# A hybrid attention and GLA layer on one core: the side work moved to another stretch of the product stream, and the blocks of x put first

## The chip, the cores and the metric

The kernel runs on one core of one Trainium2 chip. The metric is the device time of one execution in microseconds (us); the median of three runs before the change is 1817.47 us (1816.67 to 1818.06). A difference of under 0.2% (3.6 us) is taken as no change.

## What is computed

One layer, 2048 prompt tokens and 8 sequences of 8 new tokens (2112 tokens of width 1024). One wide projection gives the inputs of two branches, a sliding-window attention and a gated linear attention (GLA). Each branch is gated, projected to 1024, scaled by a sigmoid gate, and the sum is projected and normalised.

```python
z = jnp.einsum('btd,dn->btn', x, w_in)
q, k, v, g_att, gq, gk, gv, g_gla, g_lr, r_att, r_gla = jnp.split(z, SPLIT_POINTS, axis=-1)
...
    o_att = swa_prompt(q, k, v, attn_sink, rel_table)
...
log_a = jax.nn.log_sigmoid((jnp.einsum('btr,rk->btk', g_lr, w_gk_up) + b_gk)) / GATE_NORMALIZER
o_gla, S = gla(gq * HK ** -0.5, gk, gv, log_a, s0)      # causal, with a state S that is carried on
o_gla = o_gla * lax.rsqrt(jnp.mean(jnp.square(o_gla), -1, keepdims=True) + EPS) * gla_norm_w
h_att = jnp.einsum('bta,ad->btd', o_att * jax.nn.silu(g_att), w_pa)
h_gla = jnp.einsum('btv,vd->btd', o_gla * jax.nn.silu(g_gla), w_pg)
merged = jax.nn.sigmoid(r_att) * h_att + jax.nn.sigmoid(r_gla) * h_gla
y = jnp.einsum('btd,de->bte', merged, w_o)
x = layer_norm(DN_ALPHA * x + y, ln_g, ln_b)
```

## The kernel before

**Products.** The tokens are cut into three blocks (s = 0, 1, 2) of two halves of 352. Every big product is made of fp32r matmuls: each operand is split into a high and a low part (`split`, lines 141 to 145: ScalarE copies, VectorE subtracts), and `hi*hi + hi*lo + lo*hi` is three matmuls (lines 1300 to 1302). The wide projection is done in 2x2 blocks with seven products in place of eight (`ORDER`, line 50); sums of weight blocks are made on GpSimd (`tt`, line 339), sums of x blocks on VectorE (`mix`, line 452), and the partial results are put together by VectorE and ScalarE in `combine` (line 364). In block s = 0 all split weights are made here and four of seven are stored to DRAM (line 362); later blocks load those (line 319).

**Sets and the count of products.** The stream of products is a list of sets, `seq` (line 251): `x0, x1, x2` are the wide projection of a token block (177, 175 and 175 products), `a0..a2` the attention's gated projection (16 product lengths each) and `u0..u2` the GLA's (32 each). A product here is four times three matmuls of 352 columns. `base` holds the number of the product at which a set begins. The order before is x0 (0), x1 (177), a0 (352), u0 (368), x2 (400), a1 (575), u1 (591), a2 (623), u2 (639); at 671 the last projection and the norm follow.

**Side work.** Attention and GLA run between products. `at(t, fn)` (line 124) puts a step behind product t, and `tick` (line 127) runs the steps when that product has been issued. TensorE's order is this written order; the instructions of the other engines, which take their work in order too, are placed by a scheduler. `att_phase(s, t0)` (line 938) does the attention blocks of token block s, one every seven products: loads (`att_load`, line 722), the transposes of v (`att_prep`, line 748), the scores, the transposes of the weights, and the output. `gla_phase(s, t0, t1)` (line 1156) does the GLA in units of 128 tokens of a head, spread evenly over what lies between t0 and t1. A unit takes a PSUM tile `pa` (line 76) five times, of four that rotate: two transposes and scores (`gla_v`, `gla_a`), `gla_c` a third of a unit later, and two in `gla_b` at two thirds. The output of `gla_b` is held until `gla_norm` (line 1068) has been through ScalarE (the square, line 1072), GpSimd (lines 1073 and 1074) and ScalarE again (line 1075).

Before the change attention 0 begins at product 32 and GLA 0 at 80; attention 1 at 207, GLA 1 at 262; attention 2 at 430, GLA 2 at 487 to 636. The units stand 4.93, 5.73 and 5.01 products apart, from line 1161, for example (207 - 80 - 14 - 3) / (20 + 7/3) = 4.93.

**Operands of x.** `Ops.steps` (line 454) loads the four blocks of x and makes the seven split operands; `XOFF` and the other tables (lines 501 to 507) say at which product, counted from the start of the set, each step is issued. The operands live in sixteen rotating buffers `xb`, so a load waits until an operand of the set before has been used for the last time. `lowrank` (line 526) multiplies the four raw blocks with the small matrix of the GLA gate on TensorE (line 533); before, it stood in step `s7`.

Of the kernel before, what the change touches and what calls it, by code (L numbers as in the profile page):

```python
# [21 lines left out]
P = 128  # L22
# [14 lines left out]
GH = 4  # L37
# [6 lines left out]
MS = NT // (2 * MT)  # L44
# [13 lines left out]
def kernel(ctx, tc, io):  # L58
# [189 lines left out]
    px_pairs = [cx[j:j + 2] for j in range(0, 16, 2)] + [cx[16:]] + [cr[j:j + 2] for j in range(0, 8, 2)]  # L248
    two = lambda q: [[(q, 0), (q, 1)], [(q, 2), (q, 3)]]
    how = {"x": (4, px_pairs), "a": (2, two(PA_)), "u": (4, two(PG_))}  # L250
    seq = ("x0", "x1", "a0", "u0", "x2", "a1", "u1", "a2", "u2")
    sets = [(k[0], int(k[1])) + how[k[0]] for k in seq]

    groups, start_of, base = [], [], []
# [30 lines left out]
        tk += (len(groups) - start_of[-1]) * kh / 4  # L285
    start_of.append(len(groups))
    base.append(int(tk))
    X0, X1, A0, U0, X2, A1, U1, A2, U2 = range(9)
    XS = (X0, X1, X2)


# [118 lines left out]
    class Ops:  # L410
# [43 lines left out]
        def steps(self):  # L454
            r = self.r

            def s0():
                self.load(0, 0, 4 if self.n == X0 else 1)
                self.load(0, 1)

            def s1():
                self.make(1, r[0, 0], 4 if self.n == X0 else 2)

            def s2():
                self.load(1, 1)
                self.c = mtile("xb", name="cx")[:, :self.kh * T]
                self.mix(self.c, r[1, 1], r[0, 1], ALU.subtract)

            def s3():
                self.make(7, self.c)  # L470

            def s4():
                self.mix(self.c, self.c, r[0, 0], ALU.add)
                self.make(6, self.c)

            def s5():
                self.load(1, 0)

            def s6():
                self.mix(self.c, r[1, 0], self.c, ALU.subtract)  # L480
                self.make(4, self.c)

            def s7():
                if self.kind == "x":
                    lowrank(self)
                self.mix(r[0, 1], r[0, 1], r[0, 0], ALU.subtract)
                self.make(5, r[0, 1])

            def s8():
                self.make(2, r[1, 0])  # L490

            def s9():
                self.make(3, r[1, 1])

            if seq[self.n] in PLAIN:
                ld = lambda k, t: lambda: self.load(k, t)
                mk = lambda k, t: lambda: self.make((k, t), r[k, t])
                return (ld(0, 0), ld(0, 1), mk(0, 0), mk(0, 1), ld(1, 0), ld(1, 1), mk(1, 0), mk(1, 1))
            return s0, s1, s2, s3, s4, s5, s6, s7, s8, s9

    XOFF = (-18, -13, -11, -9, -7, -6, -3, 0, 1, 2)
    AOFF = (-30, -28, -24, -18, -13, -10, -6, -4, -2, 0)
    UOFF = (-16, -15, -12, -9, -4, -3, -1, 1, 2, 3)
    PX = (-18, -17, -12, -10, -8, -7, -6, -4)
    PA = (-28, -26, -24, -20, -18, -16, -12, -8)
    PU = (-16, -15, -12, -10, -8, -7, -5, -3)
# [107 lines left out]
    SU = 13  # L614
# [71 lines left out]

    at(SU, later(setup0))
    for h in range(0, NH, 2):
        at(SU + 3 + h, later(lambda h=h: setup1(h)))
    at(SU + 3, later(setup2))  # L690
    at(SU + 12, later(setup4))
    at(SU + 17, setup5)

    def gate_load(B):
        x = B["x"] = mtile("fin", name="gin")
# [242 lines left out]
    def att_phase(s, t0):  # L938
        at(t0, lambda: mpool(f"ca{s}"))
        at(t0, setup3)  # L940
        bl = ABL[s]
        for j, b in enumerate(bl):
            o = t0 + 8 + j * SB
            at(o - 7, lambda b=b: att_load(b))
            at(o - 7, lambda b=b: att_q(b))
            at(o - 1, lambda b=b: att_prep(b))
            at(o, lambda b=b: att_scores(b, 0))
            at(o, lambda b=b: att_scores(b, 2))
            at(o + 5, lambda b=b: att_sil(b))
            at(o + 6, lambda b=b: att_trans(b, 0))  # L950
            at(o + 6, lambda b=b: att_trans(b, 1))
            at(o + 9, lambda b=b: att_out(b))
        o = t0 + 8 + len(bl) * SB
        if s < MS - 1:
            return o + 5
        at(o - 4, samp_load)
        at(o + 1, samp_q)
        at(o + 2, samp_keys)
        at(o + 3, samp_rows)
        at(o + 4, lambda: samp_scores(0))  # L960
        at(o + 5, lambda: samp_scores(1))
        at(o + 9, lambda: samp_trans(0))
        at(o + 10, lambda: samp_trans(1))
        at(o + 12, samp_out)
        return o + 14
# [165 lines left out]
    def samp_b(B, j0):  # L1131
# [16 lines left out]
        for q in range(2):  # L1148
# [4 lines left out]
                                               sp[q][:, j * HV:(j + 1) * HV], ALU.mult, ALU.add)  # L1153
            b = 4 * q + j0
            nc.sync.dma_start(io["o_ss"][b:b + 2, B["h"]].rearrange("b k v -> k b v"), S0)
    def gla_phase(s, t0, t1):
        at(t0, lambda: mpool(f"cg{s}"))
        at(t0, rings)
        nu = sum(-(-T_ // P) for _, T_ in GCH[s]) * GH
        b0 = t0 + 14  # L1160
        st = (t1 - b0 - 3) / (nu + 7 / 3)
        u = 0
        for h, (c0, T_) in ([(h, c) for c in GCH[s] for h in range(GH)] if s == 1 else
                            [(h, c) for h in range(GH) for c in GCH[s]]):
            if True:
# [5 lines left out]
                b = tt(u)  # L1171
# [22 lines left out]
                    at(max(o + 6, tt(u + 4 / 3) + 1), lambda B=B: gla_store(B))  # L1194
                else:
                    at(tt(u + 7 / 3) + 1, lambda B=B: gla_store(B))

    for s in range(MS):
        for t in range(2):
            B = dict(s=s, t=t)  # L1200
            g0 = base[XS[s]] + (22 + 4 * t if s == 0 else 7 + 7 * t)
            at(g0 - 5, lambda B=B: gate_load(B))
            at(g0, lambda B=B: gate(B, 0))
            at(g0 + (s > 0), lambda B=B: gate(B, 2))
            at(g0 + 3 * (s > 0), lambda B=B: gate_end(B))
    e = att_phase(0, 32)
    for s in range(MS):
        t1 = base[XS[s + 1]] + 30 if s < MS - 1 else base[U2] - 3
        gla_phase(s, e, t1)
        if s < MS - 1:  # L1210
            e = att_phase(s + 1, t1)
    at(base[U2] + 1, lambda: mpool("cm"))


# [343 lines left out]
```

## Time and profile before

| what | value |
|---|---|
| median of the runs | 1817.47 us |
| the profiled execution, its own time | 1812.49 us |
| its span, first to last instruction | 1810.7 us |
| TensorE busy | 1767.8 us (98%) |
| VectorE, ScalarE, GpSimd busy | 1060.0, 839.0, 334.8 us |
| DMA | 452 MB, 250 GB/s on average |

The profile gives busy time per engine, waits with what ended them, and the same by stretches of time. A stretch is tied to the program by counting the matmuls of line 1300: four of them are one product of the wide projection. TensorE is the engine to watch: what it waits for is lost, and what others wait for is lost only if TensorE waits behind it. Line numbers up to 483 are the same in both kernels; behind that those of the changed kernel are 2 or 3 lower.

### The profile page before, as it was taken

The page shows a single profiled execution, that of the slowest core. Times are in us where ns is not written, and L with a number is a line of the kernel's source. Part 1 is how long each engine was busy: PE and PEld are TensorE (multiplying, and loading weights), DVE is VectorE, ACT ScalarE, POOL GpSimd, SP SyncE. Part 2 cuts the span into 40 slices and gives each one's busy share as a digit, 9 for nine tenths or more (in the row PEclk, how much of TensorE's full clock was granted, in tenths as well). Part 3 has the DMA queues.
Part 4 walks back from the last instruction along what each step waited for, and adds up shares of the span by engine and source line. Part 5 has one row for each costly group of instructions (what it writes and reads, how often), then busy time and mean ns, then how long its engine had stood idle before and what let it go on. Part 6 is the DMA issues. An engine that isn't in the chain of part 4 may idle for free.

```text
span 1810.7 us, 31028 instructions
## 1 busy us (share of the span) xinstructions
PE 1767.8 (98%) x10850; PEld 1652.0 (91%) x10850; DVE 1060.0 (59%) x2077; ACT 839.0 (46%) x1987; POOL 334.8 (18%) x473
## 2 busy tenths in 40 slices
PE   8999999998999999999999999999999999999997
PEld 8888999997898899999999998899999999998886
DVE  7577677767546654545666446554446744536665
ACT  5856555555745553445434746544445432311100
POOL 5333344554200000000034000000000022021111
PEclk9999999999999999999999999999999999999999
DMA  6789587977698779788986797788879987975531
GB/s 218 253 300 325 202 312 279 316 255 250 211 310 278 235 240 295 258 279 276 319 221 138 263 327 222 225 277 303 285 249 321 309 231 205 325 153 193 170 102 53
DMA packets 291053, 452.03 MB, mean 250 GB/s; under 512 B 29694, under 2 KB 210230, under 8 KB 290881
## 3 DMA queue, kind: packets, MB, share of 16 engines
q1 hardware_dynamic: 263536, 416.27, 69.4%
q10 hardware_dynamic: 19536, 24.47, 3.8%
q0 software_dynamic: 7824, 9.31, 3.6%
q8 instruction: 86, 1.41, 0.3%
q14 instruction: 71, 0.57, 0.1%
HBM read 297.52 MB, written 153.30 MB: 249 GB/s over the span
## 4 chain that ended last, share of the span: by engine, by line
PE 80%; DMA 6%; DVE 4%; ACT 3%; POOL 3%; issue 3%; SPq 1%; DVEq 0%; ACTq 0%; POOLq 0%
PE pd L1300 19%; PE pd L1302 18%; PE pd L1301 18%; PE pd L1364 3%; PE pd L1363 3%; PE pd L1365 3%; POOL ws L339 2%; PE pa L813 1%; PE pa L1087 1%; PE pa L1088 1%; PE pa L799 1%; PE pa L767 1%; PE pa L1085 1%; DVE wp L143 1%; DMA ws<-w_g 1%
## 5 line engine op out<-in xcount | busy, mean ns | idle before, releaser
L143 DVE TENSOR_TENSOR wp<-ws,wp 128x512 fp32r<-128x512 f32 (+1 forms) x396 | 268.7, 684 | 218.2 <-ACT wp L142 199.2
L142 ACT CAST wp<-ws 128x512 fp32r<-128x512 f32 (+1 forms) x396 | 233.0, 594 | 198.1 <-PE pd L1302 126.1
L339 POOL TENSOR_TENSOR ws<-ws 128x256 f32<-128x256 f32 x162 | 140.3, 899 | 157.9 <-DVE wp L143 111.2
L1073 POOL TENSOR_SCALAR sq<-sq 128x1 f32<-128x1 f32 x68 | 21.8, 321 | 721.8 <-ACT on L1072 721.5
L1300 PE MATMUL pd<-x7h,wp 128*128 128x352 f32 x292 | 98.6, 338 | 4.7 <-ACT fin L186 3.7
L375 ACT COPY m<-pd 128x352 f32<-128x352 f32 x146 | 65.4, 451 | 78.3 <-PE pd L1302 77.7
L1364 PE MATMUL pd<-woh,x 128*128 128x512 f32 x256 | 100.0, 391 | 0.0
L1363 PE MATMUL pd<-woh,x 128*128 128x512 f32 x256 | 99.8, 390 | 0.0
L1365 PE MATMUL pd<-wol,x 128*128 128x512 f32 x256 | 99.5, 389 | 0.0
L1300 PE MATMUL pd<-x1h,wp 128*128 128x352 f32 x292 | 97.5, 334 | 1.9 <-ACT gb L1030 1.9
L1300 PE MATMUL pd<-x2h,wp 128*128 128x352 f32 x292 | 98.2, 336 | 0.0
L1300 PE MATMUL pd<-x3h,wp 128*128 128x352 f32 x292 | 97.6, 334 | 0.6 <-DVE fin L390 0.6
L1300 PE MATMUL pd<-x4h,wp 128*128 128x352 f32 x292 | 97.6, 334 | 0.0
L1300 PE MATMUL pd<-x6h,wp 128*128 128x352 f32 x292 | 97.3, 333 | 0.0
L1300 PE MATMUL pd<-x5h,wp 128*128 128x352 f32 x292 | 96.7, 331 | 0.2 <-ACT u L379 0.2
L1302 PE MATMUL pd<-x7h,wp 128*128 128x352 f32 x292 | 94.8, 325 | 1.6 <-DVE wp L143 1.6
L1302 PE MATMUL pd<-x1h,wp 128*128 128x352 f32 x292 | 94.9, 325 | 0.0
L1301 PE MATMUL pd<-x1l,wp 128*128 128x352 f32 x292 | 94.8, 325 | 0.0
L1301 PE MATMUL pd<-x7l,wp 128*128 128x352 f32 x292 | 94.7, 324 | 0.0
L1301 PE MATMUL pd<-x3l,wp 128*128 128x352 f32 x292 | 94.6, 324 | 0.0
L1302 PE MATMUL pd<-x3h,wp 128*128 128x352 f32 x292 | 94.6, 324 | 0.0
L1302 PE MATMUL pd<-x6h,wp 128*128 128x352 f32 x292 | 94.2, 323 | 0.0
(441 smaller groups left out, 5263.2 us busy)
## 6 DMA issues: line engine op xcount, KB each, us to landing
wp<-wk_w_g SPq DMA_DIRECT2D x96, 512.0 KB
ws<-w_g SPq DMA_DIRECT2D x120, 256.0 KB
wk_w_g<-wp SPq DMA_DIRECT2D x48, 512.0 KB
wp<-wk_w_ra SPq DMA_DIRECT2D x32, 512.0 KB
wp<-wk_w_rg SPq DMA_DIRECT2D x32, 512.0 KB
ws<-w_at SPq DMA_DIRECT2D x54, 256.0 KB
wp<-wk_w_at SPq DMA_DIRECT2D x24, 512.0 KB
ws<-w_pg SPq DMA_DIRECT2D x48, 256.0 KB
```

Source lines behind the costliest of these rows:

```text
L142: pin["a"] = nc.scalar.copy(dst_h, src)
L143: i = eng.tensor_tensor(dst_l, src, dst_h.bitcast(F32), ALU.subtract)
L339: nc.gpsimd.tensor_tensor(o[:, c], x[:, c], y[:, c], op)
L375: nc.scalar.copy(A[i], ps)
L767: mm(ps[kv][:, j, k0:], A["zq"][r, g0 + j, :], A["kk"][r, 0, k0:], start=True, stop=True, tile_position=(kv * HD, 0))
L1073: nc.gpsimd.tensor_scalar(sq[:n], sq[:n], EPS, None, op0=ALU.add)
L1300: mm(ps, wh, xh[:, ts], start=first, stop=False, skip_group_check=ch)
L1301: mm(ps, wh, xl[:, ts], start=False, stop=False, skip_group_check=ch)
L1302: mm(ps, wl, xh[:, ts], start=False, stop=(k == q.kh - 1 and not (type(i) is tuple and i[1] == 0)), skip_group_check=ch)
L1363: mm(ps, xh[:, xs], hi, start=(k == 0), stop=False)
L1364: mm(ps, xl[:, xs], hi, start=False, stop=False)
L1365: mm(ps, xh[:, xs], lo, start=False, stop=(k == KT - 1))
```

## The change

- `seq`: x2 now stands ahead of a0 and u0: x0 (0), x1 (177), x2 (352), a0 (527), u0 (543), a1 (575), u1 (591), a2 (623), u2 (639).
- Side work: attention 0 begins at product 90 in place of 32, and all GLA units of the three blocks have one distance, (636 - 90 - 160 - 51) / 75 = 4.47 products. By that, attention 0 begins at 90, GLA 0 at 138, attention 1 at 254, GLA 1 at 309, attention 2 at 443, GLA 2 at 500 (to 634).
- The setup of the bias and the first two gates stand further apart (gates at 40 and 52 in place of 22 and 26).
- `att_prep` stands three products ahead of the scores in place of one; the load of `kk` stays seven ahead.
- `XOFF`: the seven operands of x1 and x2 are made later and further apart; `lowrank` moves to 2 products ahead of the set (from the set's first product), while the load of the last raw block moves from 6 to 3 ahead.

```diff
-    seq = ("x0", "x1", "a0", "u0", "x2", "a1", "u1", "a2", "u2")
+    seq = ("x0", "x1", "x2", "a0", "u0", "a1", "u1", "a2", "u2")
...
             def s7():
-                if self.kind == "x":
-                    lowrank(self)
                 self.mix(r[0, 1], r[0, 1], r[0, 0], ALU.subtract)
                 self.make(5, r[0, 1])
...
-            return s0, s1, s2, s3, s4, s5, s6, s7, s8, s9
-
-    XOFF = (-18, -13, -11, -9, -7, -6, -3, 0, 1, 2)
-    AOFF = (-30, -28, -24, -18, -13, -10, -6, -4, -2, 0)
-    UOFF = (-16, -15, -12, -9, -4, -3, -1, 1, 2, 3)
+            return s0, s1, s2, s3, s4, s5, s6, s7, s8, s9, lambda: lowrank(self)
+
+    XOFF = (-18, -12, -9, -6, -4, -3, 0, 3, 5, 7, -2)
+    AOFF = (-30, -28, -24, -18, -13, -10, -6, -4, -2, 0, -5)
+    UOFF = (-16, -13, -10, -7, -4, -3, 0, 3, 5, 7, -2)
...
-        at(SU + 3 + h, later(lambda h=h: setup1(h)))
+        at(SU + 5 + 4 * h, later(lambda h=h: setup1(h)))
     at(SU + 3, later(setup2))
-    at(SU + 12, later(setup4))
-    at(SU + 17, setup5)
+    at(SU + 32, later(setup4))
+    at(SU + 38, setup5)
...
-            at(o - 1, lambda b=b: att_prep(b))
+            at(o - 3, lambda b=b: att_prep(b))
...
-    def gla_phase(s, t0, t1):
+    def gla_phase(s, t0, st):
...
-        st = (t1 - b0 - 3) / (nu + 7 / 3)
...
+        return int(b0 + st * (nu + 7 / 3) + 3)
...
-            g0 = base[XS[s]] + (22 + 4 * t if s == 0 else 7 + 7 * t)
+            g0 = base[XS[s]] + (40 + 12 * t if s == 0 else 7 + 7 * t)
...
-    e = att_phase(0, 32)
+    t0 = 90
+    tiles = [sum(-(-n // P) for _, n in c) * GH for c in GCH]
+    st = (base[U2] - 3 - t0 - 160 - 17 * MS) / sum(n + 7 / 3 for n in tiles)
     for s in range(MS):
-        t1 = base[XS[s + 1]] + 30 if s < MS - 1 else base[U2] - 3
-        gla_phase(s, e, t1)
-        if s < MS - 1:
-            e = att_phase(s + 1, t1)
+        t0 = gla_phase(s, att_phase(s, t0), st)
```

Three places show how the instructions stand now. The first is VectorE where x1's operands begin, some nine products ahead of product 177. `wp` is a split weight, `ws` its raw block, `cx` the difference of two raw x blocks, `r11` the block whose load it needs; `S`, `gb`, `dm` and `e1` belong to the GLA. Before:

```order
L1093 SCALAR_TENSOR_TENSOR S1_218<-S3_220,e1_4431,pa_5056 128x256
L143 TENSOR_TENSOR wp_5065<-ws_4756,wp_5065 128x512
L1032 COPY e1_5156<-gb_5145 128x2
L1045 SCALAR_TENSOR_TENSOR gb_5145<-zkq_5008,gb_5145 128x256
L452 TENSOR_TENSOR cx_5051<-r11_5049,r01_4836 128x704 x2
L1065 COPY_PREDICATED aper0_206<-cmask_199,pa_5088 128x128
L143 TENSOR_TENSOR wp_5095<-ws_4972,wp_5095 128x512
L143 TENSOR_TENSOR x7l_5114<-cx_5051,x7h_5113 128x704
```

VectorE at the same place of the changed kernel:

```order
L143 TENSOR_TENSOR wp_4631<-ws_4318,wp_4631 128x512
L1013 SCALAR_TENSOR_TENSOR gb_4923<-rmask_202,gin_4741 128x256
L1018 TENSOR_TENSOR dm_4925<-gb_4923 128x256
L143 TENSOR_TENSOR wp_4651<-ws_4536,wp_4651 128x512
L1091 SCALAR_TENSOR_TENSOR S2_219<-S1_218,e1_4220,pa_4676 128x256
L452 TENSOR_TENSOR cx_4671<-r11_4669,r01_4392 128x704 x2
L143 TENSOR_TENSOR wp_4689<-ws_4558,wp_4689 128x512
L384 TENSOR_TENSOR fin_4705<-u2_4647,pd3_77 128x352
```

The split that reads the raw block which GpSimd overwrites next (`ws_4972` before, `ws_4536` now) stood behind the difference `cx`, and now stands ahead of it.

The second place is GpSimd at the same point: `sq` is the GLA's norm, the other rows are sums of weight blocks. Before:

```order
L1073 TENSOR_SCALAR sq_5060<-sq_5060 128x1
L1074 TENSOR_TENSOR sq_5060<-sq_5060,mhalf_205 128x1
L339 TENSOR_TENSOR ws_4972<-ws_4972,ws_4657 128x256 x2
L339 TENSOR_TENSOR w7_5317<-ws_5093,ws_5158 128x256 x2
L339 TENSOR_TENSOR ws_5158<-ws_5158,ws_5229 128x256 x2
L339 TENSOR_TENSOR ws_5010<-ws_5010,ws_4698 128x256 x2
L339 TENSOR_TENSOR w7_5341<-ws_5119,ws_5192 128x256 x2
L339 TENSOR_TENSOR ws_5192<-ws_5192,ws_5256 128x256 x2
L1073 TENSOR_SCALAR sq_5224<-sq_5224 128x1
L1074 TENSOR_TENSOR sq_5224<-sq_5224,mhalf_205 128x1
```

GpSimd at that point of the changed kernel:

```order
L339 TENSOR_TENSOR ws_4536<-ws_4536,ws_4240 128x256 x2
L1071 TENSOR_SCALAR sq_4680<-sq_4680 128x1
L1072 TENSOR_TENSOR sq_4680<-sq_4680,mhalf_205 128x1
L339 TENSOR_TENSOR w7_4875<-ws_4649,ws_4717 128x256 x2
L339 TENSOR_TENSOR ws_4717<-ws_4717,ws_4783 128x256
L339 TENSOR_TENSOR ws_4558<-ws_4558,ws_4260 128x256 x2
L339 TENSOR_TENSOR ws_4717<-ws_4717,ws_4783 128x256
L339 TENSOR_TENSOR w7_4936<-ws_4687,ws_4745 128x256 x2
L339 TENSOR_TENSOR ws_4745<-ws_4745,ws_4814 128x256 x2
L339 TENSOR_TENSOR ws_4649<-ws_4717,ws_4649 128x256 x2
L1071 TENSOR_SCALAR sq_4809<-sq_4809 128x1
L1072 TENSOR_TENSOR sq_4809<-sq_4809,mhalf_205 128x1
```

A norm still stands behind twelve sums, but the first two of the burst now stand ahead of the norm before it.

The third place is TensorE at `lowrank`; `r_5216` and `r_4865` are the raw block that is loaded last. Before, it follows the first product of x1 on its operand `x1`:

```order
L1301 MATMUL pd_77<-x1l,wp 128x352
L1302 MATMUL pd_77<-x1h,wp 128x352
L533 MATMUL pa<-r_4834,wg 32x352
L533 MATMUL pa<-r_4836,wg 32x352
L533 MATMUL pa<-r_5216,wg 32x352
L533 MATMUL pa<-r_5049,wg 32x352
```

In the changed kernel it follows the second-last product of x0, on x0's operand `x3`:

```order
L1299 MATMUL pd_75<-x3l,wp 128x352
L1300 MATMUL pd_75<-x3h,wp 128x352
L531 MATMUL pa<-r_4390,wg 32x352
L531 MATMUL pa<-r_4392,wg 32x352
L531 MATMUL pa<-r_4865,wg 32x352
L531 MATMUL pa<-r_4669,wg 32x352
```

`lowrank` came two products earlier against the release of the buffer that its last block is loaded into, since that release hangs on the products of x0 and did not move.

More of the change, by code (lines that the diff above doesn't have):

```diff
@@ L287 @@
     base.append(int(tk))
-    X0, X1, A0, U0, X2, A1, U1, A2, U2 = range(9)
+    X0, X1, X2, A0, U0, A1, U1, A2, U2 = range(9)
     XS = (X0, X1, X2)
@@ L1205 @@
             at(g0 + 3 * (s > 0), lambda B=B: gate_end(B))
-    e = att_phase(0, 32)
+    t0 = 90
+    tiles = [sum(-(-n // P) for _, n in c) * GH for c in GCH]
+    st = (base[U2] - 3 - t0 - 160 - 17 * MS) / sum(n + 7 / 3 for n in tiles)
     for s in range(MS):
-        t1 = base[XS[s + 1]] + 30 if s < MS - 1 else base[U2] - 3
-        gla_phase(s, e, t1)
-        if s < MS - 1:
-            e = att_phase(s + 1, t1)
+        t0 = gla_phase(s, att_phase(s, t0), st)
+    assert t0 <= base[U2] - 2
     at(base[U2] + 1, lambda: mpool("cm"))
```

## The prediction

> **What bounds the kernel now.** I read the page first, for the share of each engine.
>
> ```profile
> span 1810.7 us, 31028 instructions
> PE 1767.8 (98%) x10850; PEld 1652.0 (91%) x10850; DVE 1060.0 (59%) x2077; ACT 839.0 (46%) x1987; POOL 334.8 (18%) x473
> ```
>
> TensorE is the bound, and the change neither adds nor removes a matmul. What can move is the 1810.7 - 1767.8 = 42.9 us in which TensorE is idle, and stretches in which it runs slowly. So I read next the busy time by stretch (columns: stretch, its length, then the busy time and count of PE, PEld, DVE, ACT, POOL, the granted clock, the DMA share, GB/s), and in a second table the matmuls of line 1300 alone, which count the products.
>
> ```profile
> 24.70:85.20 60.50, 56.80 (x359) 51.06 (x357) 41.26 (x61) 42.11 (x82) 25.05 (x31) 1.00 0.56 191
> 85.20:212.70 127.50, 123.32 (x774) 111.35 (x775) 92.60 (x169) 76.74 (x206) 40.52 (x51) 0.99 0.81 283
> 212.70:449.80 237.10, 222.75 (x1365) 216.97 (x1364) 168.97 (x308) 131.60 (x309) 119.45 (x150) 0.99 0.81 281
> 665.90:864.20 198.30, 198.30 (x1245) 195.94 (x1244) 95.85 (x207) 94.43 (x222) 10.37 (x24) 1.00 0.87 282
> 864.20:975.90 111.70, 109.48 (x684) 107.43 (x684) 67.31 (x136) 42.41 (x96) 30.44 (x43) 1.00 0.83 238
> 1195.60:1401.80 206.20, 206.20 (x1298) 197.43 (x1296) 107.58 (x262) 97.28 (x229) 12.58 (x31) 1.00 0.87 289
> 1401.80:1556.60 154.80, 152.74 (x956) 143.82 (x955) 83.92 (x204) 51.73 (x125) 24.52 (x41) 1.00 0.86 258
> 1616.10:1810.70 194.60, 184.19 (x845) 153.52 (x844) 118.20 (x192) 22.77 (x48) 27.96 (x27) 0.99 0.42 133
> ```
>
> ```profile
> 0.00:85.20 85.20, 43.55 (x129) 25.12 (x129) 1.00 0.67 227
> 85.20:212.70 127.50, 64.05 (x193) 36.76 (x193) 0.99 0.81 283
> 212.70:449.80 237.10, 131.10 (x388) 73.61 (x387) 0.99 0.81 281
> ```
>
> Four such matmuls are a product, so these three end at products 32, 80 and 177: the start of attention 0, its end, and the end of x0. Idle time: 3.7 us between 24.7 and 85.2 (gates and setup of the bias), 4.2 in attention 0, 14.4 in GLA 0 under x0. GLA 1 in x1 (665.9 to 864.2) and GLA 2 in x2 (1195.6 to 1401.8) lose nothing; a0 with u0, and a1, u1, a2 (864.2 to 975.9, 1401.8 to 1556.6), lose 2.2 and 2.1. The last stage's 10.4 is outside the change. So the loss sits in x0, where all weights are made: GpSimd is busy half of GLA 0's stretch (119.45 of 237.1) and VectorE 71%; later blocks load most weights.
>
> The waits of TensorE name the causes (total us, times, longest):
>
> ```profile
> PE pa L1102 <- ACT on L1075: 5.3, 1, 5.3
> PE pd L1300 <- ACT fin L186: 3.7, 1, 3.7
> PE pa L1063 <- DVE sg L1104: 3.0, 1, 3.0
> PE pd L1302 <- DVE wp L143: 1.6, 1, 1.6
> PE pa L753 <- DMA kk<-z_kv: 0.9, 1, 0.9
> PE pa L753 <- ACT pT L803: 0.8, 2, 0.5
> ```
>
> The 5.3 and 3.0 stand together, just ahead of product 177. The timeline of SP, VectorE, GpSimd and ScalarE there:
>
> ```profile
> 419.56 0.39 SPq L431 DMA_DIRECT2D r<-xT  x1
> ...
> 426.19 1.69 DVE L452 TENSOR_TENSOR cx<-r,r 128x704 f32<-128x704 f32 x2 [4.32 <-DMA r<-xT]
> ...
> 428.76 2.65 POOL L339 TENSOR_TENSOR ws<-ws 128x256 f32<-128x256 f32 x2 [7.62 <-DVE wp L143]
> ...
> 442.36 0.22 POOL L1073 TENSOR_SCALAR sq<-sq 128x1 f32<-128x1 f32 x1
> ...
> 443.26 0.47 ACT L1075 ACTIVATE on<-pa,sq 128x256 f32<-128x256 f32 x1 [1.86 <-POOL sq L1074]
> ```
>
> x1's operand load is issued at 419.56; VectorE stands 4.32 us on it at `cx`; the weight split behind `cx` comes late, GpSimd stands 7.62 us on that, then runs its twelve sums in one go (13 us), and the GLA's norm behind them leaves at 442.36. TensorE needs the PSUM tile that this norm holds.
>
> The long waits also cost clock: three stretches at half clock.
>
> ```profile
> 84.75:88.16 3.41, 2.97 (x10) 2.97 (x11) 3.41 (x5) 2.58 (x7) 2.17 (x3) 0.50 1.05 395
> 303.20:306.61 3.41, 3.41 (x13) 3.41 (x13) 3.41 (x7) 1.86 (x4) 3.41 (x5) 0.50 0.16 59
> 443.15:446.56 3.41, 2.77 (x10) 2.77 (x11) 2.08 (x5) 2.90 (x7) 2.51 (x5) 0.50 1.03 366
> ```
>
> Matmuls in them start 0.29 us apart, elsewhere 0.16 (twelve, a product, take 1.92):
>
> ```profile
> 85.94 0.49 PE L1302 MATMUL pd<-x7h,wp 128*128 128x352 f32 x1
> 86.23 0.49 PE L1300 MATMUL pd<-x7h,wp 128*128 128x352 f32 x1
> ...
> 502.73 0.32 PE L1300 MATMUL pd<-x4h,wp 128*128 128x352 f32 x1
> ...
> 504.65 0.32 PE L1300 MATMUL pd<-x4h,wp 128*128 128x352 f32 x1
> ```
>
> Some ten matmuls times 0.13 is 1.3 us a stretch, 3.9 in all.
>
> **The change part by part: what goes.** Up to 3.7 + 4.2 + 14.4 + 3.9 = 26.2 us lie in x0.
>
> Products 32 to 90 lose their side work, and gates and setup are spread: of the 3.7 us I leave 0.5 (between 0, as in the stretches without loss, and 3.7).
>
> Attention 0 still runs under x0, with the same load. Its 4.2 are mostly the weight split (1.6), the load of `kk` (0.9) and two kinds of waits of the transposes of v for PSUM tiles that the transposes just ahead of them hold (0.8 of them is quoted). The last go, since `att_prep` now stands three products ahead of the scores and not behind those transposes. I leave 2.5 (between 1.6 and 4.2).
>
> GLA 0 overlaps x0 for the 25 products from 152 to 177, not 97. The 14.4 less the pair 5.3 + 3.0 is 6.1 over the 84 products ahead of that pair: 13 of them remain, 0.9 us. The pair itself sits at x0's end, where GLA 0 still is. Its cause is weakened, not gone: VectorE still stands on `r11`, whose buffer comes free as before, but the split that GpSimd needs now stands ahead of `cx`, so GpSimd can begin its sums some 4 us earlier. Against that, the norm still has twelve sums ahead of it. Between 0 and 8.3 I take 3. One stretch of half clock may stay: 1.0.
>
> Left in x0: 0.5 + 2.5 + 0.9 + 3.0 + 1.0 = 7.9. Gain: 26.2 - 7.9 = 18.3.
>
> **What is new.** (1) `lowrank` stands two products earlier, its last load no earlier, for its buffer is freed by x0's products: the lead is three products, 5.8 us by the 1.92 above. What such loads take:
>
> ```profile
> 1.65 4.49 DMA r<-xT
> 904.98 7.82 DMA r<-xT
> ```
>
> The first is a quarter of a block, the second a whole one, and the one of 419.56 took about 6.6. So x1 and x2 each wait between 0 and some 3 us (7.82 + 1 of issue - 5.8); I take 0.8 each, 1.6. Queued behind TensorE's wait are only its own products; nobody else waits. By the Trainium skill (DMA: Bandwidth & Descriptors, Anatomy of one DMA, fitted on the GpSimd path) a transfer takes about 2.0 us plus its bytes over 436 GB/s, an estimate of 3.7 us for 704 KB, and this term would be 0; the trace's 6.6 and 7.82 are longer, and the measurement decides.
>
> (2) The transposes of v come two products, 3.8 us, earlier against the load of `kk`, which stays. At the first block of attention 0 TensorE already waits for it:
>
> ```profile
> 97.03 0.65 SPq L730 DMA_DIRECT2D kk<-z_kv  x1
> ...
> 103.07 0.30 PE L753 MATMUL pa<-ident,kk 128*128 128x128 f32 x1 [0.91 <-DMA kk<-z_kv]
> ```
>
> That is 6.0 us from issue to use. Only the first block of each phase has its load so close. Three of them, each between 0 and 3.8 us: I take 1.0 each, 3.0.
>
> (3) The gated projections lose 2.2 + 2.1 now; with GLA 2 at 4.47 products a unit over all of them (a0 and u0 had 5.73) I add 1.0, between 0 and another 4.3.
>
> (4) GLA 1 and 2 at 4.47: a norm's PSUM tile is wanted again after two thirds of a unit, 3.0 products in place of 3.3 to 3.8. GLA 1 and 2 show no wait at those, so the margin is unknown; 1.5 us, between 0 and 8.3, the pair of x0.
>
> (5) Operands made later cost nothing, their cover being 5 or more products (9.6 us) between making and use, against 1.69 us for a `cx` of two pieces and as much again for a split; if that cover went, each would cost what the load costs, 4.3 us. x2 ahead of a0 moves work without changing it.
>
> New: 1.6 + 3.0 + 1.0 + 1.5 = 7.1. Net: 18.3 - 7.1 = 11.2 us. The profiled execution (span 1810.7, its own time 1812.49, so 1.8 around the span) would have a span of about 1799.5 and a time of 1801.3; the median of the runs is 1817.47, 5 us above it, and goes to about 1806.
>
> A rule weighed: by the Trainium skill (TensorE: Matmul & The Clock Gate, HAM oscillation) the clock halves only when idle gaps are longer than some 3.4 us; then the new waits of 1 us cost no clock. The stretch at 303.2 speaks against it in part, since no wait over 2 us stands ahead of it there; if each new wait cost a stretch of 1.3 us, five would add 6.5 and the sum would be 1812.
>
> **The rivals.**
>
> *Nearly all of the idle time goes.* The norm is no longer late at x0's end, loads land in time: 26.2 less 1.6 for a weight split left, and none of the new terms: 1817.5 - 24.6 = 1793. For it: the stretches without weight making lose nothing. Against: the twelve sums are still there. Chance 0.20.
>
> *The loss only moves.* The pair at x0's end stays in full with its stretch of clock (5.3 more than I leave), `lowrank` waits 3 us twice (4.4 more): 11.2 - 9.7 = 1.5 us of gain, 1816. For it: the load of `r11` is tied to x0's products, so that making operands "later" does not make them later; in this part the change may not do what it says. Chance 0.14.
>
> *The even distance is too short, and it is slower.* One mechanism: the norm goes TensorE, ScalarE, GpSimd, ScalarE, and holds a PSUM tile of four. ScalarE waits for GpSimd in it:
>
> ```profile
> ACT on L1075 <- POOL sq L1074: 92.6, 68, 6.9
> ```
>
> This is 1.4 us on average, 6.9 at worst. If the chain takes longer than the 3.0 products, 5.8 us and the side work between, every unit makes TensorE wait. At 0.5 us for each of 68 units it costs 34 us, against 18.3 less 5.6 of other new terms: 21 us slower, 1839; it decides from 0.2 us a unit. Against it: at 4.93 and 5.01 products most norms had three whole products as well, and the stretch at 1195.6 lost nothing. Chance 0.08.
>
> **How the numbers follow.** The forecast as worked out has 0.58. The time is 1806. The range 1795 to 1819 takes in the bounds of the x0 terms (gain of 26.2 less part of the new ones; or 1.5 gained and the unknown terms near their ends); about 0.1 lies on each side. Faster by over 0.2% (3.6 us): the forecast, nearly all of it, and the first rival, 0.77. Within: the second rival and little of the others, 0.14. Slower: 0.09. Under 0.2% a measurement of this kernel can't tell from no change.
>
> **What would show it.** Right: no waits between products 32 and 90; one wait of 2 to 4 us near product 175; short waits at `lowrank` (line 531) on `r<-xT` and at line 751 on `kk`; at most one half-clock stretch ahead of the last stage. Wrong: waits of line 1100 on line 1073 spread over GLA 1 and 2; `lowrank` waiting over 3 us; or waits of products on weight splits in attention 0 longer than 4 us.

## The result and the profile after

The changed kernel takes 1805.82 us (median of ten runs, 1797.66 to 1812.69), the kernel before 1814.90 us (ten runs, 1812.29 to 1818.77). The ratio is 0.9950, 95% interval 0.9936 to 0.9963: 9.1 us are gained, between 7 and 12. The profiled execution of the changed kernel took 1804.37 us, its span is 1802.6 us against 1810.7.

The page first, for the share of each engine:

```profile
span 1802.6 us, 31059 instructions
PE 1768.2 (98%) x10850; PEld 1651.8 (92%) x10850; DVE 1059.3 (59%) x2077; ACT 844.2 (47%) x1989; POOL 344.0 (19%) x473
```

TensorE is as busy as before (1768.2 against 1767.8 us), so the gain is idle time: 34.4 us in place of 42.9. The stretches say where. Cut by the count of products, they are products 8 to 32, 32 to 90, attention 0 (90 to 138), GLA 0 under x0 (138 to 177), GLA 0 under x1 (177 to 254), GLA 1 under x2 (352 to 443), a0 with u0 (527 to 575), and a1, u1, a2 (575 to 639). Columns as before: stretch, length, busy time and count of PE, PEld, DVE, ACT, POOL, granted clock, DMA share, GB/s.

```profile
25.40:77.30 51.90, 51.90 (x335) 48.93 (x334) 38.49 (x53) 23.82 (x47) 28.24 (x33) 1.00 0.58 206
77.30:198.40 121.10, 117.61 (x722) 114.67 (x720) 71.69 (x106) 75.06 (x149) 54.76 (x64) 0.99 0.87 301
198.40:320.70 122.30, 121.62 (x776) 110.20 (x775) 94.14 (x171) 77.68 (x207) 47.61 (x56) 1.00 0.81 283
320.70:412.60 91.90, 87.81 (x560) 83.81 (x560) 69.66 (x117) 54.67 (x123) 47.26 (x56) 1.00 0.86 290
412.60:600.00 187.40, 185.14 (x1135) 177.53 (x1134) 93.66 (x207) 101.60 (x236) 22.31 (x40) 1.00 0.82 260
...
839.00:1059.60 220.60, 218.56 (x1350) 210.83 (x1349) 106.55 (x226) 118.51 (x267) 21.47 (x46) 1.00 0.79 258
...
1263.00:1387.90 124.90, 122.54 (x770) 113.67 (x770) 79.92 (x204) 50.53 (x124) 26.00 (x41) 1.00 0.87 254
1387.90:1548.40 160.50, 157.20 (x974) 148.14 (x973) 85.24 (x209) 52.07 (x126) 26.43 (x45) 0.99 0.85 249
```

Length less PE busy is the loss of each: 0, 3.5, 0.7, 4.1, 2.3, 2.0, 2.4 and 3.3 us. x0 now loses 8.3 us in place of 22.2, and GLA 0 and GLA 1 under the later blocks lose 4.3, where the kernel before lost 0.9. The waits of TensorE (total us, times, longest) name what is left:

```profile
...
PE pd L1298 <- DVE fin L396: 3.9, 3, 2.6
PE pa L531 <- DMA r<-xT: 2.9, 1, 2.9
...
PE pd L1298 <- DVE fin L219: 2.3, 1, 2.3
PE pa L1061 <- DVE sg L1102: 1.8, 2, 1.0
```

The pair ahead of product 177 has gone: no wait of line 1102 (now 1100) on the norm is in the list, and the 1.8 us of line 1063 (now 1061) for `sg` lie elsewhere, under the gated projections (0.8 us at 1325 and 1.0 at 1395). No wait of line 751 for `kk` is there either, and `lowrank` waits once, 2.9 us. The timeline around x0's end shows why the pair is no longer seen (engines mixed, in order of time; in brackets the idle time ahead and what ended it):

```profile
388.12 1.43 POOL L339 TENSOR_TENSOR ws<-ws 128x256 f32<-128x256 f32 x2 [8.08 <-DVE wp L143]
...
391.39 1.96 DVE L452 TENSOR_TENSOR cx<-r,r 128x704 f32<-128x704 f32 x2 [2.96 <-DMA r<-xT]
...
402.45 0.64 SPq L431 DMA_DIRECT2D r<-xT  x1
...
406.83 0.47 ACT L1073 ACTIVATE on<-pa,sq 128x256 f32<-128x256 f32 x1 [3.30 <-POOL sq L1072]
...
407.87 2.56 PE L531 MATMUL pa<-r,wg 128*32 128x352 f32 x28 [2.94 <-DMA r<-xT]
...
410.36 0.44 PE L1100 MATMUL pa<-ident,on 128*128 128x128 f32 x2
```

GpSimd takes up its sums 3.3 us ahead of `cx`, where before it stood behind it by 2.6. The norm still leaves late (407.3), but TensorE stands at `lowrank` until 407.87, for a load issued at 402.45, and works on it until 410.4; the norm's tile is free by then, so nothing of its lateness is seen.

Two stretches of half clock lie ahead of the last stage, three before:

```profile
136.49:139.90 3.41, 3.41 (x14) 3.41 (x13) 3.41 (x4) 2.38 (x6) 3.14 (x4) 0.50 0.95 354
1542.80:1546.21 3.41, 3.09 (x11) 3.12 (x12) 2.84 (x6) 0.56 (x2) 0.00 (x0) 0.50 0.95 332
```

The longest wait in x0 that the prediction did not have is that for `fin` (line 396), 2.6 us, just ahead of the first of these stretches. ScalarE and VectorE there:

```profile
128.34 1.28 ACT L713 ACT_TABLE_LOAD   x1
...
130.17 3.46 DVE L716 SCALAR_TENSOR_TENSOR mg<-mg,zg 128x352 f32<-128x352 f32 x4 [4.57 <-ACT zg L713]
...
131.83 1.28 ACT L194 ACT_TABLE_LOAD   x1
...
134.68 0.94 DVE L396 TENSOR_TENSOR fin<-m,pd 128x352 f32<-128x352 f32 x2
```

This is the second gate, now at product 52: its instructions on ScalarE come in one go with a table load on either side, VectorE stands 4.57 us on them at line 716, and behind that stands the sum that frees TensorE's product tile. The weight load of the same product waits 2.87 us as well, until 135.30, for a split that stands behind the gate on ScalarE; which of the two let TensorE go on isn't told apart.

### The profile page after: what moved, and what is told of

Its sections match the earlier page's. It is cut to its first block, busy times and chain, and to the rows that moved or that the text cites. A ratio compares the mean times of both kernels' runs of the same rounds, so it can differ in the third digit from the quotient of the medians.

```text
span 1802.6 us, 31059 instructions
## 1 busy us (share of the span) xinstructions
PE 1768.2 (98%) x10850; PEld 1651.8 (92%) x10850; DVE 1059.3 (59%) x2077; ACT 844.2 (47%) x1989; POOL 344.0 (19%) x473
## 4 chain that ended last, share of the span: by engine, by line
PE 68%; DMA 4%; ACT 3%; DVE 2%; issue 1%; POOL 1%; SPq 0%; DVEq 0%; ACTq 0%; POOLq 0%
PE pd L1298 15%; PE pd L1300 15%; PE pd L1299 15%; PE pd L1362 3%; PE pd L1361 3%; PE pd L1363 3%; DMA r<-ug_d 1%; PE pa L1085 1%; PE pa L1086 1%; PE pa L1083 1%; PE pa L765 1%; PE pa L811 1%; PE pa L797 1%; PE pa L1100 1%; PE pa L1051 1%
## 5 line engine op out<-in xcount | busy, mean ns | idle before, releaser
L1298 PE MATMUL pd<-x5h,wp 128*128 128x352 f32 x292 | 97.8, 335 | 0.0
L1298 PE MATMUL pd<-x2h,wp 128*128 128x352 f32 x292 | 97.2, 333 | 0.0
L1300 PE MATMUL pd<-x2h,wp 128*128 128x352 f32 x292 | 94.2, 323 | 0.0
L1300 PE MATMUL pd<-x5h,wp 128*128 128x352 f32 x292 | 94.2, 323 | 0.0
```

Of the source, the lines that this page charges most:

```text
L1298: mm(ps, wh, xh[:, ts], start=first, stop=False, skip_group_check=ch)
L1300: mm(ps, wl, xh[:, ts], start=False, stop=(k == q.kh - 1 and not (type(i) is tuple and i[1] == 0)), skip_group_check=ch)
```

## The experiments

The theory: the gain comes from the side work that leaves the stretch in which all weights are made, and the rest of the change only makes that possible or costs a little. Each run was compared with the kernel before on the same chip; times are medians, ratios are to the kernel before.

**The side work back at 32.** The changed kernel with the old start, and with setup and gates where they were; the units stand (636 - 32 - 211) / 75 = 5.24 products apart.

```diff
-    t0 = 90
+    t0 = 32
...
-            g0 = base[XS[s]] + (40 + 12 * t if s == 0 else 7 + 7 * t)
+            g0 = base[XS[s]] + (22 + 4 * t if s == 0 else 7 + 7 * t)
```

> The changed kernel with side work from product 32 on at one even distance (5.24 products a unit), and with the setup of the bias and the first gates where they were before. Theory: the gain is side work that has left x0, so most of it goes: x0 again loses some 20 us to waits and half clock against some 8 in the changed kernel, and the time is 1814 to 1819, 8 to 13 us over the changed kernel. Rival (the gain comes from x2 standing ahead of a0, or from the operands): the time stays within 3 us of the changed kernel's 1806.

Measured: 1826.94 us, 1.0066 (1.0047 to 1.0085), some 21 us behind the changed kernel, and slower than the kernel before. Six half-clock stretches lie ahead of the last stage. Products 32 to 90, and the waits:

```profile
87.60:242.00 154.40, 146.36 (x893) 133.64 (x894) 109.53 (x191) 86.29 (x226) 57.15 (x67) 0.97 0.79 272
```

```profile
PE pd L1298 <- ACT fin L186: 5.7, 2, 3.7
...
PE pa L751 <- DMA kk<-z_kv: 4.4, 1, 4.4
PE pa L1100 <- ACT on L1073: 2.9, 1, 2.9
```

8.0 us lost here, against 3.5 in the changed kernel; loads of `kk`, the gates and the norm make TensorE wait again. The direction is the theory's, the size isn't: 8 us above the range expected, and 12 us slower than the kernel before, which has the same start. Setup and gates are back here too, so the 21 us aren't the start's alone, and why the other parts are worth less than nothing at this start is open.

**The order of the sets alone.** The kernel before with the new `seq`; the second and third attention start where they did.

```diff
-    seq = ("x0", "x1", "a0", "u0", "x2", "a1", "u1", "a2", "u2")
+    seq = ("x0", "x1", "x2", "a0", "u0", "a1", "u1", "a2", "u2")
...
-        t1 = base[XS[s + 1]] + 30 if s < MS - 1 else base[U2] - 3
+        t1 = (207, 430)[s] if s < MS - 1 else base[U2] - 3
```

> The kernel before with x2 ahead of a0 and u0 as the only change; the side work keeps its products (32, 80, 207, 262, 430, 487). Theory: moving the sets moves work without changing it, so the time is within 3 us of the kernel before (1812 to 1818), x0 loses the same 22 us. Rival (the order of the sets carries the gain): 1807 or less.

Measured: 1816.95 us, 1.0017 (1.0001 to 1.0032). No gain, as the theory expected; x0 loses 19.4 us, not the 22 expected. The first wait of the pair is there unchanged:

```profile
PE pa L1102 <- ACT on L1075: 5.3, 1, 5.3
```

The counterpart, the later start in the old order, wasn't tried and can't be as it stands. u0 reads tokens up to 704, and GLA 0 ends at token 640 (`GCH`, line 47): the rest comes from the first units of GLA 1. These begin at 309 + 14 = 323 and would be stored at about 323 + 4.47 x (8 + 7/3) + 1 = 370, too late for u0 at product 368. So the order is worth nothing by itself and is what lets the side work start at 90.

**`lowrank` later.** In the changed kernel, `lowrank` goes back from 2 products ahead of the set to 2 behind its start.

```diff
-    XOFF = (-18, -12, -9, -6, -4, -3, 0, 3, 5, 7, -2)
+    XOFF = (-18, -12, -9, -6, -4, -3, 0, 3, 5, 7, 2)
```

> The changed kernel with lowrank four products later (2 behind the set's first product in place of 2 ahead). Theory: the wait of 2.9 us on the last raw block goes and nothing comes in its place: 1802 to 1804, no wait at line 531. Rival: that wait covers GpSimd's norm, which ends only some 1 us earlier in the profile; without it TensorE waits 2 to 3 us for the PSUM tile of the norm (lines 1061 or 1100) near product 176, and the time stays at 1805 to 1807.

Measured: 1805.60 us, 0.9949 (0.9933 to 0.9966), the same as the changed kernel. The wait for the load is gone and the time is not; TensorE waits for other things:

```profile
PE pa L1061 <- DVE sg L1102: 6.0, 3, 3.3
...
PE pa L531 <- DVE S L1091: 1.7, 1, 1.7
```

At the place itself, products 138 to 207, TensorE loses 6.1 us in place of 6.4 (the stretch takes 170.5 us, in the changed kernel 171.6): with the 2.9 us gone, 1.1 come due at line 1061, 0.6 at line 1100 and 1.7 at `lowrank`, all for PSUM tiles. So the wait at `lowrank` covered others, as the rival has it, though none of these is on the norm that it named. The other 4.9 us of line 1061 stand far from there, under the gated projections.

**`att_prep` back.** The transposes of v again one product ahead of the scores.

```diff
-            at(o - 3, lambda b=b: att_prep(b))
+            at(o - 1, lambda b=b: att_prep(b))
```

> The changed kernel with the transposes of v back at one product ahead of the scores. Theory: the load of kk was in time in the changed kernel (no wait on it), so nothing is won; the waits on the PSUM tiles of the transposes just ahead come back, 0.8 to 1.6 us in attention 0: 1806 to 1808. Rival: the place of the transposes does nothing, or each of the 13 extra switches between product and transpose costs something and the time falls to 1803 or less.

Measured: 1811.19 us, 0.9977 (0.9964 to 0.9989), some 5 us behind the changed kernel. Attention 0 and the wait that came back in it:

```profile
195.80:321.90 126.10, 122.40 (x775) 110.09 (x774) 94.47 (x171) 77.94 (x207) 47.01 (x56) 1.00 0.78 269
```

```profile
PE pa L751 <- ACT pT L801: 2.5, 3, 1.7
```

The stage loses 3.7 us in place of 0.7 and is 3.8 us longer; of the wait shown, 1.7 us, once, lie in it. So the distance of `att_prep` bears on attention 0's loss, but not alone: two runs below that leave it as it is lose 3.2 and 1.7 us there.

**Starts at 70 and 110.** The rest as in the changed kernel; the distance follows from the start, 4.73 and 4.20 products.

```diff
-    t0 = 90
+    t0 = 70
```

> The changed kernel with side work from product 70 on (4.73 products a unit). GLA 0 then overlaps x0 for 45 products in place of 25. Theory (overlap with x0 costs): from start 32, which overlaps 97 products and is 21 us slower than the changed kernel, some 0.3 us a product, so 5 to 6 us slower than it: 1810 to 1813. Rival (the shorter distance of units costs): 4.73 has more room than 4.47, and the time falls to 1803 or less.

```diff
-    t0 = 90
+    t0 = 110
```

> The changed kernel with side work from product 110 on (4.20 products a unit); GLA 0 overlaps x0 for 5 products. Theory (overlap costs): 2 to 5 us faster than the changed kernel, 1801 to 1804. Rival (distance costs): a norm's PSUM tile is wanted after 2.8 products, often only two whole ones; waits at lines 1061, 1085 and 1100 in GLA 1 and 2, and 1810 or more.

Measured: 1820.99 us, 1.0041 (1.0027 to 1.0055), and 1817.50 us, 1.0014 (1.0001 to 1.0027). Both are over 11 us behind the start at 90. The start at 70 loses in products 32 to 90, where part of attention 0 now lies:

```profile
76.50:211.20 134.70, 126.16 (x771) 119.73 (x770) 83.61 (x134) 82.05 (x186) 53.90 (x64) 0.97 0.84 291
```

8.5 us. In all of x0 it loses 18.0, against 8.3 in the changed kernel and 23.7 with the start at 32. The start at 110, with 11.4 in x0, loses 10.9 us far from there, under a0 and u0 (products 527 to 575; 2.4 in the changed kernel):

```profile
1264.70:1402.50 137.80, 126.89 (x772) 117.97 (x772) 76.77 (x192) 50.84 (x125) 25.46 (x42) 0.98 0.85 249
```

The timeline of ScalarE, VectorE and TensorE there:

```profile
1338.37 0.78 ACT L142 CAST x(0, 1)h<-r 128x704 fp32r<-128x704 f32 x1 [7.27 <-DMA r<-ug_d]
...
1340.70 0.33 PE L1100 MATMUL pa<-ident,on 64*128 64x64 f32 x2 [2.51 <-ACT gv L1053]
...
1348.27 0.69 DVE L1013 TENSOR_TENSOR_SCAN gb<-rmask,gin 128x256 f32<-128x256 f32 x1 [6.16 <-DMA gin<-zg_d]
...
1349.80 0.28 DVE L1102 TENSOR_TENSOR sg<-pa,sg 128x128 f32<-128x128 f32 x1
...
1350.13 0.80 PE L1061 MATMUL pa<-dm,em 128*128 128x128 f32 x2 [5.35 <-DVE sg L1102]
```

ScalarE stands 7.27 us on the load of a gated projection's operand, a copy of the GLA (`gv`) stands behind it, and TensorE waits 2.51 us for the tile that this copy reads. Then VectorE stands 6.16 us on the load of `gin`, until 1348.27, and TensorE 5.35 us on a tile that VectorE frees right behind that. So behind each of these two waits stands a late load, not a unit that comes too soon. That the rows hang together is read from their order; no run changed a load alone. Both expectations by overlap missed: the start at 70 cost 15 us and not 5 to 6, and the start at 110 gained nothing; there the rival holds as far as its time and the tiles of lines 1061 and 1100 go.

**Only the distance.** To part the start from the distance: start 90, distance 4.20.

```diff
-    st = (base[U2] - 3 - t0 - 160 - 17 * MS) / sum(n + 7 / 3 for n in tiles)
+    st = 4.20
```

> The changed kernel with attention 0 at product 90 as it is, but the GLA's units 4.20 products apart in place of 4.47, so that GLA 2 ends some 20 products earlier. It separates the start from the distance: the start at product 110 had both a later start and 4.20. Theory (the distance itself costs, through units that follow each other too closely while TensorE does a0 and u0, where products are short): as with the start at 110, idle time between products 527 and 575 rises from 2.4 to 8 to 11 us and the time is 1814 to 1818, against 1815 for the kernel before. Rival (the late start cost, or the place at which the units met the gated projections): within 3 us of the changed kernel, 1803 to 1809, and no more than 4 us idle between 527 and 575.

Measured: 1821.32 us, 1.0039 (1.0026 to 1.0051): a distance of 4.20 costs without the later start. The place is only half as expected (products 177 to 207, then 527 to 575):

```profile
412.30:500.00 87.70, 80.25 (x471) 73.35 (x469) 52.39 (x118) 59.32 (x136) 16.73 (x24) 0.98 0.73 234
1281.60:1413.80 132.20, 126.49 (x781) 117.78 (x779) 77.72 (x198) 50.19 (x122) 25.10 (x42) 0.97 0.86 253
```

7.5 us go at the start of x1 (2.3 in the changed kernel) and 5.7 under a0 and u0, in waits of many lines. With the distance every later unit, and attention 1 and 2, also fall at other products; whether the closeness itself costs or what they now meet, the run doesn't part.

**Operands earlier.** The changed kernel with the old offsets of x's operands, `lowrank` one product ahead of the set.

```diff
-    XOFF = (-18, -12, -9, -6, -4, -3, 0, 3, 5, 7, -2)
+    XOFF = (-18, -13, -11, -9, -7, -6, -3, 0, 1, 2, -1)
```

> The changed kernel with the operands of x1 and x2 made at the old products, lowrank at 1 ahead of the set so that it still reads the raw blocks. Theory: the loads hang on the release of buffers by the products of the set before, so making operands later was worth little: within 3 us of 1806. Rival: the old places put four operands into three products and again put the difference cx ahead of the split that GpSimd waits for; the pair of waits at x0's end comes back, 5 to 8 us: 1811 to 1814.

Measured: 1809.71 us, 0.9976 (0.9964 to 0.9989), 4 to 5 us behind the changed kernel. Part of the pair is back, 4.0 of these 6.9 us, just ahead of product 177:

```profile
PE pa L1061 <- DVE sg L1102: 6.9, 3, 4.0
```

**Operands later, alone.** The kernel before with the new tables of offsets only (those of the gated projections too, and `lowrank` as its last step).

```diff
-    XOFF = (-18, -13, -11, -9, -7, -6, -3, 0, 1, 2)
+    XOFF = (-18, -12, -9, -6, -4, -3, 0, 3, 5, 7, -2)
```

> The kernel before with the new offsets of the operands alone (made later and further apart, the last load and lowrank earlier); sequence and side work as before. Theory (by the run that put the old offsets into the changed kernel, 4 us worse): the pair of waits ahead of product 177, 5.3 and 3.0 us, falls to half or less; a lowrank wait of some 3 us comes; 1811 to 1813 against 1815 for the kernel before. Rival (as the prediction had it, making operands later is worth nothing): the pair stays at 6 us or more, and with lowrank the time is 1815 to 1818.

Measured: 1815.26 us, 1.0005 (0.9993 to 1.0017): no change, as the rival had it. Waits are moved, not removed:

```profile
PE pa L1100 <- DVE S L1091: 3.5, 1, 3.5
PE pa L531 <- ACT on L1073: 3.1, 1, 3.1
```

The second is on the tile that the norm holds: `lowrank` now meets it, in place of line 1102. The other of the pair is 2.35 us in place of 3.0. The 3.5 us stand some 90 us ahead of them, where 1.7 were lost before. So later operands give 4 to 5 us in the changed kernel and nothing without the moved side work.

**Gates and setup back.** In the changed kernel, both at the products of the kernel before.

```diff
-            g0 = base[XS[s]] + (40 + 12 * t if s == 0 else 7 + 7 * t)
+            g0 = base[XS[s]] + (22 + 4 * t if s == 0 else 7 + 7 * t)
```

> The changed kernel with the setup of the bias and the two first gates at the products of the kernel before (gates at 22 and 26 in place of 40 and 52). Theory (this term was sized at 3.7 less 0.5 us and a stretch of half clock): the wait of products on fin at line 186 ahead of product 32 comes back with 3 to 4 us and a half-clock stretch of 1.3, the 2.6 us near product 58 goes, so 1 to 3 us more than the changed kernel, 1807 to 1809. Rival (the side work from 32 on was what made the gates late, not their spacing): idle time up to product 90 is at or below 3.5 us and the time is 1803 to 1806.

Measured: 1811.47 us, 0.9989 (0.9973 to 1.0005), between 5 and 7 us behind the changed kernel, more than the 1 to 3 expected:

```profile
PE pd L1298 <- ACT fin L186: 3.7, 1, 3.7
...
PE pa L765 <- ACT pT L801: 2.2, 2, 1.4
```

The 3.7 us are back to the tenth, with a stretch of half clock behind them, and the 3.5 us between products 32 and 90, with theirs, are gone: product 90 is reached at 198.9 us in place of 198.4. So in its own place the spacing is worth 0.5 us. The rest comes later: attention 0, which the edit doesn't touch, loses 3.2 us in place of 0.7, 2.2 of it at line 765, and takes 4.0 us more. Why it does is open.

**Gates in steps.** The two halves of the first gates one and three products apart, as those of later blocks are.

```diff
-            at(g0 + (s > 0), lambda B=B: gate(B, 2))
-            at(g0 + 3 * (s > 0), lambda B=B: gate_end(B))
+            at(g0 + 1, lambda B=B: gate(B, 2))
+            at(g0 + 3, lambda B=B: gate_end(B))
```

> The changed kernel with the steps of the first two gates one and three products apart, as those of later blocks are, in place of all at one product. Theory: the wait of 2.6 us near product 58 is VectorE standing on ScalarE's sixteen gate instructions and two table loads in one go, with the products' sums behind; apart they leave room, and the wait and its stretch of half clock (1.3) go: 1802 to 1804. Rival: ScalarE's work is the same and the wait stays at 2 to 3 us: 1805 to 1807.

Measured: 1808.58 us, 0.9969 (0.9955 to 0.9983): no gain. The waits for `fin` of line 396 are down to 0.7 us from 3.9, and others stand in the list; the 2.2 at line 186 end at 138.77, near the second gate's last steps, with a stretch of half clock 0.6 us behind them:

```profile
PE pa L1100 <- DVE S L1150: 2.6, 1, 2.6
...
PE pd L1298 <- ACT fin L186: 2.2, 1, 2.2
...
PE pd L1298 <- DVE fin L396: 0.7, 1, 0.7
```

The steps also bring ScalarE six table loads of 1.28 us for the two gates in place of four, so the run doesn't test the one go alone.

**The norm's tile freed early.** The kernel before, with one more copy on ScalarE behind the norm's square, so that GpSimd no longer stands between the output and the release of its PSUM tile.

```diff
         nc.scalar.activation(on[:n], o, AF.Square, scale=1.0 / 16, accum_out=sq[:n])
+        nc.scalar.copy(on[:n], o)
...
-        nc.scalar.mul(on[:n], o, sq[:n])
+        nc.scalar.mul(on[:n], on[:n], sq[:n])
```

> The kernel before with one more ScalarE copy in the GLA's norm: the output of gla_b is copied out of PSUM right behind the square, and the last multiplication works in place, so that the PSUM tile is free before GpSimd has done its two steps. 68 copies of about 0.5 us on ScalarE are added. Theory as the prediction has it (TensorE waits ahead of product 177 for the PSUM tile that the norm holds): the pair of 5.3 and 3.0 us goes, ScalarE's copies lie beside other work, 1807 to 1810 against 1815. Rival (line 1102 transposes the norm's result, and waits for that as its data, whoever holds the tile): the wait at line 1102 stays at 4 to 6 us, and the time is 1815 to 1819.

Measured: 1811.65 us, 0.9988 (0.9975 to 1.0002): 2.8 us by the medians, not told from none by the interval. The place decides. The square of that norm in the kernel before, whose tile is free at 443.73 by the row of line 1075 in the prediction:

```profile
440.55 0.37 ACT L1072 ACTIVATE on<-pa 128x256 f32<-128x256 f32 x1
```

The same norm with the copy (lines behind it are one higher):

```profile
439.17 0.62 ACT L142 CAST wp<-ws 128x512 fp32r<-128x512 f32 x1 [4.16 <-POOL ws L339]
...
441.29 0.37 ACT L1072 ACTIVATE on<-pa 128x256 f32<-128x256 f32 x1
...
442.04 0.36 ACT L1073 COPY on<-pa 128x256 f32<-128x256 f32 x1
...
442.45 0.44 PE L1103 MATMUL pa<-ident,on 128*128 128x128 f32 x2 [0.58 <-ACT on L1073]
...
443.12 0.22 POOL L1074 TENSOR_SCALAR sq<-sq 128x1 f32<-128x1 f32 x1
```

TensorE goes on right behind the copy, 0.67 us before GpSimd begins that norm: this wait was for the tile, as the prediction says, and not for the norm's result; the rival is wrong. The other of the pair, for `sg`, stays, 3.25 us at 434.87. The tile is free 1.1 us after the square begins (441.29 to 442.40) in place of 3.2, so GpSimd's steps are 2 us of the hold. The rest lies ahead of the square: ScalarE stands 4.16 us at a weight split that waits for GpSimd's sums, with the square queued behind it. That the wait falls from 5.3 to 0.6 us isn't all gain: TensorE comes to it later, after 6.83 us of half clock from 433.91 on, and GLA 0 under x0 (products 80 to 177) is 1.9 us shorter, 235.3 against 237.2.

## Why the prediction was right, and where not

The direction and the size were right: 1806.0 forecast, 1805.82 measured; a gain of 11.2 us forecast for the profiled execution, 8.1 in the two spans, 9.1 in the medians (the base of 1817.47 us was 2.6 above the median of all ten runs). That the time is met to 0.2 us is luck: a gain forecast 2.1 too large and a base 2.6 too high cancel, and below several terms are off both ways. Point by point:

- **Side work out of products 32 to 90: shown.** It was put at 18.3 us with all that goes with it. In the profile, x0 loses 26.2 - 6.6 = 19.6 us less, with 2.9 at `lowrank` counted below. What TensorE loses in x0 follows the start: 23.7 us at 32, 18.0 at 70, 8.3 at 90. The 21 us of the start at 32 hold the gates too.
- **"Of the 3.7 us I leave 0.5": the step failed.** Products 8 to 32 lose nothing, but 32 to 90 lose 3.5 and a stretch of half clock. The prediction took the spacing of the gates for their cost, but in its place the spacing moves the loss and hardly lessens it: 3.9 us up to product 90 without it, 3.5 with it, a stretch of half clock in both. In the trace the loss stands behind a gate that runs on ScalarE in one go; the run with steps in between still loses 2.2 us there and doesn't settle it. That the whole is 5 to 7 us worse without the spacing comes from later stages, and isn't explained.
- **Attention 0, 2.5 left: 0.7 measured.** The cause named is part of it: with `att_prep` back 3.7, of which 1.7 is the wait named. With the gates back it is 3.2 though `att_prep` stays.
- **GLA 0 under x0, 0.9 and the pair at 3.0: 1.2 for both.** The mechanism named is shown for the longer of the two (sums ahead of `cx`, a tile held by a norm that stands behind the sums); the wait for `sg` stays when that tile is freed early, and its cause isn't shown. The sum missed that the pair and `lowrank` lie in the same place and cover each other: 3.0 and 1.6 were added, and one wait of 2.9 us is what came. The run with `lowrank` later shows it: 3.4 us of waits for tiles come due in its stead.
- **`lowrank`, 0.8 twice: 2.9 and 0.** Within its bounds in the one block; in the other the load was in time. By the rule weighed there, of the Trainium skill (DMA: Bandwidth & Descriptors, Anatomy of one DMA), the load would be an estimated 3.7 us and this term 0; here it was 5.4 us from issue to use, and the measurement decides.
- **The load of `kk`, 3.0: nothing.** The prediction let the load stay at its product. In the changed kernel the first load leaves at 196.7, before product 90 is through, and its first use is at 209.9 (first start to last start in the rows of these two lines):

```profile
L728 SPq DMA_DIRECT2D kk<-z_kv x16: 518/533/947, 196.7 to 1116.6; - x16
...
L751 PE MATMUL pa<-ident,kk x31: 270/272/273, 209.9 to 1145.8; 128*128 128x128 f32 x31
```

  13.2 us lie between them, where 6.0 lay before. The written product is the earliest place in the order, and how far SP's queue runs behind or ahead of TensorE sets the rest: in the crowded stretch from 32 on it ran late (the load left at 97.03, product 32 ended at 85.2), at 90 it does not.
- **The even distance, 1.5 and the gated projections 1.0: 4.3 and 1.4, with a stretch of 1.3.** The sizes are within their ranges, the mechanism of the first isn't: it was the norm's tile wanted too soon, and of the 4.3 us only 0.4 is a wait on the norm (line 1061 on line 1073); the rest is for `aper` (1.5), `gv` (0.7) and the sum of line 390 (1.6). That a distance of 4.20 loses the gain is shown by the start at 110 and by 4.20 with the start at 90, 15 us worse than the changed kernel and 7 us slower than the kernel before. So a loss like the third rival's comes a quarter of a product lower, at a third of its price of 21 us, but not by its mechanism: the wait it would show by, line 1100 on line 1073, is not among the larger ones in either run.
- **"Operands made later cost nothing" stands; that they bring little does not.** They are worth 4 to 5 us here, and nothing in the kernel before.
- **Half clock: one stretch forecast in the text, two came.** The rule of the Trainium skill that was weighed (TensorE: Matmul & The Clock Gate, HAM oscillation), that it takes idle gaps over some 3.4 us, isn't borne out: the waits at both were 2.6 and 2.3 us.

In sum: left in x0 6.6 us (forecast 7.9), new 2.9 + 4.3 + 1.4 + 1.3 = 9.9 (forecast 7.1), net 26.2 - 6.6 - 9.9 = 9.7. The 0.9 that the kernel before lost in its later blocks goes as well: 10.6. The spans differ by 8.1; 0.7 of the rest is the first stretch (25.4 us to product 8 against 24.7), 1.8 are not accounted for.

**What stays open.** Parts put back singly cost 21 (the start, with gates), 5 (`att_prep`), 4 to 5 (operands) and 5 to 7 us (gates), far more together than the 9.1 gained, and 20 products of start either way cost over 11. The parts hold each other up, and the changed kernel stands in a narrow place: how much of its time is a rule and how much a lucky fit of steps that don't meet, these runs don't tell. None of the versions tried is measurably faster.

## What to carry to other kernels

When the bound engine loses its time in one crowded stretch, move the movable work out of that stretch before mending single waits there; a reorder that is worth nothing alone may be what makes room for it. Waits that lie in one place cover each other, so add the longest of them, and not all; take one away, and look for what comes due behind it. Start and spacing have edges: here 4.47 products a unit from product 90 gained 9 us, 4.20 lost it all, and so did 4.73 from product 70, so a start that is moved must be tried on both sides. Sum a wait by its place, not by its line: the same line can wait hundreds of microseconds away for another reason.

## What the runs showed of the hardware

- Every stretch of half clock ahead of the last stage was 3.41 us long in both kernels; in the other runs some were 6.83, twice that (433.91 to 440.74 with the norm's tile freed early). In the changed kernel one began 1.2 us behind the end of a wait of 2.61 us, one 0.3 us ahead of the end of a wait of 2.29 us, while the wait of 2.94 us at `lowrank` had none behind it: the length of the last wait alone does not decide.
- The kernel before spread over 6 us in its ten runs, the changed one over 15; but 35 other runs of the kernel before spread over 16 (1808.6 to 1824.7). With 6 runs of a version the interval here is 3 us to each side (`lowrank` later), with 12 some 2.2 (operands later, alone).
